# Opening by quarters, filler matmuls in TensorE's waits, and normalized tokens stored in the order in which the gather loads them

## The chip, the cores and the metric

One core of a Trainium2 chip (eight cores, two dies of four) runs the whole kernel. The metric is device time of one execution in microseconds (us), lower is better, as the median of three runs. All inputs lie in HBM and the output goes back there; all arithmetic is fp32, or fp32 split into parts.

## The reference

A decoder trunk of two layers over 256 tokens of width 1024. For each layer:

```python
mod = cond @ w_mod[l] + b_mod[l]                 # cond = silu(c): one row, 6 x 1024 columns
sh1, sc1, g1, sh2, sc2, g2 = split(mod, 6)
h = layer_norm_plain(x) * (1 + sc1) + sh1
q, k, v, p = split(h @ w_in[l], 4)               # 512 columns each
a = moba_attention(rope(q), rope(k), v)          # 256 tokens are one block: causal attention, 8 heads
m = pool_mixer(p, w_pool[l], pool_scale[l])      # trailing means over 2, 4, 8, 16 tokens
x = layer_norm_affine(ALPHA * x + g1 * (concat(a, m) @ w_out[l]), ln1_g[l], ln1_b[l])
h = layer_norm_plain(x) * (1 + sc2) + sh2
y = grouped_moe(h, ...)                          # router, then 2 of 16 SwiGLU experts for each token
x = layer_norm_affine(ALPHA * x + g2 * y, ln2_g[l], ln2_b[l])
```

The weights are some 280 MB in fp32, all read once; the 16 experts of a layer (1024x512 gate and up, 512x1024 down) are the largest part.

## The kernel before

Tokens are held as two halves of 128 partitions (t = 0, 1). All large weights come through one stream (class `Stream`, L35 to L71): a list of pieces in a fixed order, each a DMA of up to 1 MiB issued from the SP queue into a ring of 21 slots of [128, 2048] fp32. A new piece goes out when its slot has been given back; `st.free` in the program says from where on, and on the chip SP waits for the last reader of the slot. Scratch tiles (`slot()`) come from the same ring. The order of every engine's instructions is that of the program (a manual schedule), so an instruction that waits holds up all that stand behind it on its engine. PSUM has eight banks, `ps()`.

A layer runs like this. `mod01` (L301; layer 0) multiplies the conditioning with the columns of shift 1 and scale 1, in two halves h of 512 columns; `mod01_fin` (L314) copies the result, transposes it and adds the biases, which gives columns `col01`. `plain` (L389) normalizes a token half into `xn`; `enter` (L410) transposes xn and applies scale and shift, which gives `hT`. `qk_mm` (L428) multiplies hT with the q and k columns of w_in, for a token half t and a quarter q of the contraction. In layer 0, `ready(h)` does the first three steps for half h and stands before the two quarters that need it (L445). Then `row_parts` (L259) splits rows of constants, and `mod_dve` (L350) forms a modulation row on DVE (VectorE): eight multiply-adds (L356, L358) over [128, 1024]. `rope` (L702) turns parts of q and k on DVE. TensorE (PE) multiplies the pool columns (L478), `pool` (L716) sums windows on POOL (GpSimd), and q and k are transposed (L501) and copied (L502, half of the copies on DVE), scores (L508, L513), softmax, `v` (L552), output projection `out_mm` (L596), `norms_of(t)` (L607) with an affine norm and a plain norm (L391 through `plain`) that writes `xn2[t]`.

The router path follows: `turn(t)` (L620) transposes xn2, logits, `exps`; xn2 is split into `xh` and `xl` (two fp32r parts); `gate()` spreads g2 (L344, L345); `router` picks experts on DVE (L750 to L778), counts places with small matmuls (L784 to L789), and `onehot` (L821) forms the selection matrices. `gather(i)` (L835) then collects the tokens of eight experts: for each k of 8 it multiplies a 128x128 block of xh or xl, taken as the stationary operand with a step of eight columns, with the selection:

```python
T.matmul(b, xs[:, t, k::8], SX[i][t], start=(n == 0), stop=(n == 3))      # L843
```

The experts run as eight pairs (L1035): `gate_up` (L885), `silu`, `act_t` (L905, transposes and an ACT copy), `down` (L922), `combine` (L947). The last pair adds into four banks XB that are kept; statistics of them (L940, L943) stand at the end of `down`, and the closing norm (`norm`, `norm_aside`, L1065 to L1087) is applied in the next layer's `ready` or, at the end, just before the output's DMAs (L1120 to L1123).

## Time and profile before

| | us |
|---|---|
| three runs | 734.01, 729.12, 731.86 (median 731.86) |
| the profiled execution | 732.26 |
| its span on the core | 730.5 |

Over the span PE is busy 675.4 us (92%), DVE 323.9, ACT 127.7, POOL 46.9; the mean DMA rate is 384 GB/s, and HBM reads are 278.59 MB. PE's busy time is no measure of its load: matmuls are pipelined and their ends are modelled. The profile's parts that are used here: the windows view (busy time of each engine, granted TensorE clock, share of the 16 DMA engines and GB/s in a stretch), the timeline (instructions in order of time, with the idle time ahead of each and what ended it), the waits of a queue, and groups by line. PEld is the weight load of a matmul. A granted clock of 1.00 is 2.4 GHz, 0.50 is 1.2 GHz; a value between is a mean over both.

### The profile page before, as it was taken

The page shows a single profiled execution, that of the slowest core. Times are in us where ns is not written, and L with a number is a line of the kernel's source. Part 1 is how long each engine was busy: PE and PEld are TensorE (multiplying, and loading weights), DVE is VectorE, ACT ScalarE, POOL GpSimd, SP SyncE. Part 2 cuts the span into 40 slices and gives each one's busy share as a digit, 9 for nine tenths or more (in the row PEclk, how much of TensorE's full clock was granted, in tenths as well). Part 3 has the DMA queues.
Part 4 walks back from the last instruction along what each step waited for, and adds up shares of the span by engine and source line. Part 5 has one row for each costly group of instructions (what it writes and reads, how often), then busy time and mean ns, then how long its engine had stood idle before and what let it go on. Part 6 is the DMA issues. An engine that isn't in the chain of part 4 may idle for free. (4 is left out here: it accounts for less than half of the span.)

```text
span 730.5 us, 8092 instructions
## 1 busy us (share of the span) xinstructions
PE 675.4 (92%) x3101; PEld 322.0 (44%) x3101; DVE 323.9 (44%) x572; ACT 127.7 (17%) x274; POOL 46.9 (6%) x74
## 2 busy tenths in 40 slices
PE   4899799979899999999979999997999999998994
PEld 1347455544333363333324575555434345332331
DVE  2117898652243343232253876665332342342315
ACT  0111332122001121101102125213210111111100
POOL 4000500100000000000000041010000000000001
PEclk9999899999999999999999999997999999999998
DMA  9999999798999999999999999967599999999992
GB/s 325 395 391 408 410 370 379 282 415 323 423 422 419 421 421 423 421 417 418 398 408 390 409 410 415 372 266 309 216 423 421 422 421 421 421 418 421 418 399 91
DMA packets 57633, 280.36 MB, mean 384 GB/s; under 512 B 5009, under 2 KB 6073, under 8 KB 34537
## 3 DMA queue, kind: packets, MB, share of 16 engines
q1 hardware_dynamic: 56944, 279.20, 94.8%
q8 instruction: 29, 0.48, 0.3%
q10 hardware_dynamic: 312, 0.32, 0.1%
q0 software_dynamic: 320, 0.14, 0.1%
q14 instruction: 28, 0.22, 0.1%
HBM read 278.59 MB, written 1.05 MB: 383 GB/s over the span
## 5 line engine op out<-in xcount | busy, mean ns | idle before, releaser
L885 PE MATMUL ps<-wr 128*64 128x512 f32 x1024 | 224.3, 593 | 0.0
L885 PEld LDWEIGHTS ps<-wr 128*64 128x64 f32 x1024 | 73.1, 137 | 145.6 <-issue 140.7
L922 PE MATMUL ps<-wr,s 128*64 128x512 f32 x512 | 115.3, 602 | 4.0 <-ACT s L910 4.0
L922 PEld LDWEIGHTS ps<-wr,s 128*64 128x64 f32 x512 | 36.1, 138 | 73.3 <-issue 64.0
L932 DVE SCALAR_TENSOR_TENSOR s<-ps,gc,gb 128x512 f32<-128x512 f32 x32 | 23.9, 748 | 89.0 <-PE ps L922 89.0
L434 PE MATMUL ps<-wr,hT 128*128 128x512 f32 x128 | 56.9, 603 | 0.9 <-ACT hT L423 0.6
L596 PE MATMUL ps<-wr,hT 128*128 128x512 f32 (+1 forms) x160 | 55.7, 507 | 0.0
L358 DVE SCALAR_TENSOR_TENSOR wr<-wr,condT 128x1024 f32<-128x1024 f32 x42 | 54.2, 1290 | 2.3 <-DMA wr<-in_w_mod_dram 0.8
L935 ACT CAST wr<-s 128x512 fp32r<-128x512 f32 x30 | 18.5, 618 | 167.1 <-PE ps L885 109.1
L902 DVE TENSOR_TENSOR s<-s,ps 128x512 f32<-128x512 f32 x16 | 11.0, 687 | 79.4 <-PE ps L885 79.4
L936 DVE TENSOR_TENSOR wr<-s,wr 128x512 fp32r<-128x512 f32 x30 | 20.8, 692 | 55.6 <-ACT wr L935 50.8
L596 PEld LDWEIGHTS ps<-wr,hT 128*128 128x128 f32 x160 | 30.2, 190 | 23.8 <-issue 21.3
L434 PEld LDWEIGHTS ps<-wr,hT 128*128 128x128 f32 x128 | 24.4, 194 | 31.0 <-issue 28.5
L947 PE MATMUL ps<-wr,sT 128*128 128x512 f32 x120 | 33.6, 412 | 0.0
L910 ACT COPY s<-ps 128x512 f32<-128x512 f32 x16 | 9.4, 587 | 135.4 <-PE ps L908 135.4
L843 PE MATMUL ps<-s,xn 128*128 128x512 f32 x64 | 28.9, 451 | 2.1 <-DVE s L821 2.1
L1085 POOL TENSOR_TENSOR rs<-rs,mhalf 128x2 f32<-128x2 f32 x2 | 1.4, 702 | 457.1 <-DVE rs L1084 457.1
L552 PE MATMUL ps<-wr,hT 128*128 128x512 f32 x64 | 28.3, 596 | 0.0
L947 PEld LDWEIGHTS ps<-wr,sT 128*128 128x128 f32 x120 | 20.9, 189 | 16.3 <-issue 13.0
L478 PE MATMUL ps<-hT,wr 128*128 128x256 f32 x128 | 28.1, 380 | 0.0
L843 PE MATMUL ps<-s,hT 128*128 128x512 f32 x64 | 27.6, 431 | 0.0
L478 PEld LDWEIGHTS ps<-hT,wr 128*128 128x128 f32 x128 | 24.2, 190 | 4.5 <-issue 1.3
(236 smaller groups left out, 627.2 us busy)
## 6 DMA issues: line engine op xcount, KB each, us to landing
wr<-in_w_gate_dram SPq DMA_DIRECT2D x64, 1024.0 KB, 18.2
wr<-in_w_up_dram SPq DMA_DIRECT2D x60, 1024.0 KB, 18.8
wr<-in_w_down_dram SPq DMA_DIRECT2D x56, 1024.0 KB, 18.7
wr<-in_w_mod_dram SPq DMA_DIRECT2D x48, 1024.0 KB, 14.6
wr<-in_w_in_dram SPq DMA_DIRECT2D x16, 1024.0 KB, 16.7
wr<-in_w_out_dram SPq DMA_DIRECT2D x8, 1024.0 KB, 18.6
wr<-in_w_down_dram SPq DMA_DIRECT2D x12, 512.0 KB, 11.1
wr<-in_w_up_dram SPq DMA_DIRECT2D x8, 512.0 KB, 17.4
```

The lines of the kernel that those rows point to most:

```text
L358: V.scalar_tensor_tensor(acc, w[:, kk], condT[:, k, 0:1], acc, op0=OP.mult, op1=OP.add)
L434: T.matmul(pq[t][n], hT[:, k, t * 128:(t + 1) * 128], w[:, kk, n * 512:(n + 1) * 512], start=(k == 0), stop=(k == 7))
L478: T.matmul(pp[g // 2][:, (g % 2) * 256:(g % 2) * 256 + 256], w[:, kk, g * 128:(g + 1) * 128], hT[:, k, :], start=(k == 0 and g % 2 == 0), ...
L552: T.matmul(pv[t], hT[:, k, t * 128:(t + 1) * 128], w[:, kk, :], start=(k == 0), stop=(k == 7))
L596: T.matmul(py[t][-1][:, 0:c1 - c0], catT[:, k, t * 128:(t + 1) * 128], w[:, kk, n * 512 + c0:n * 512 + c1], start=(q == 2 and kk == 0), st ...
L843: T.matmul(b, xs[:, t, k::8], SX[i][t], start=(n == 0), stop=(n == 3))
L885: T.matmul(bs[nm][64 * j:64 * j + 64, :], XE[i][k // 4][:, k % 4, c0:c0 + 64], st.get((nm, l, 2 * i + j, q))[:, k - k0, :], start=(k == 0) ...
L922: T.matmul(bo[n][64 * j:64 * j + 64, :], AT[i][:, k, 64 * j:64 * j + 64], st.get(("d", l, 2 * i + j, q))[:, k - k0, (n - n0) * 512:(n - n0 ...
L932: V.scalar_tensor_tensor(o, bo[n], GC[i], g2[:, c0], op0=OP.mult, op1=OP.mult)
L935: A.copy(oh[:, c0], o)
L936: V.tensor_sub(ol[:, c0], o, oh[:, c0].bitcast(F))
L947: T.matmul(b, STt[i][:, t * 128:(t + 1) * 128], o[:, n * 512:(n + 1) * 512], start=(start and j == 0), stop=(stop and j == 1), skip_group_ ...
```

## The change

- **Opening by quarters.** The mod01 pieces become four quarters of 256 columns (contiguous runs of 1 KB in HBM where they were 2 KB), each followed by one qk piece; x's second half follows the first quarter. `ready` goes by quarters: mod01 of the next quarter is issued before the second token half of the quarter at hand, and `enter01` transposes both token halves into one bank.
- **Filler matmuls.** `warm(n)` issues n matmuls of constant ones (bf16, 128x512) whose result nobody reads, at eight places, 2 to 10 at a time.
- **Order of xn2.** `norms_of` writes the normalized tokens regrouped (column q*8+k of x goes to place k*128+q), with a strided read on DVE. turn and gather (and `over`) then read runs of 128 columns in place of steps of eight.
- **Smaller moves.** The small loads on POOL's queue come after the constants; mod_dve(2) comes after rope in layer 0; `mod_fin(l+1, 1)` one pair later; act_t of the first and last pair is shared between DVE and ACT; the closing statistics are taken for each token half on its own (`ends(t)`), the second inside the first one's norm.

```diff
     def add_mod01(h):
         w = w_mod[0].rearrange("(p k) n -> p k n", k=8)
-        for q in range(2):
-            for v in range(2):
-                st.add(("m01", h, q, v), w[:, 4 * q:4 * q + 4, v * D + h * 512:v * D + (h + 1) * 512])
+        for v in (1, 0):
+            st.add(("m01", h, v), w[:, :, v * D + h * 256:v * D + (h + 1) * 256])
...
-    for h in range(2):
+    for h in range(4):
         add_mod01(h)
         if not h:
             load_x(1)
-        add_qk(0, 2 * h)
-        add_qk(0, 2 * h + 1)
+        add_qk(0, h)
...
+    def warm(n):
+        b = ps().rearrange("p (a c) -> p a c", a=4)
+        for _ in range(n):
+            T.matmul(b, ones, ones[:, None, :].to_broadcast([128, 4, 128]), start=True, stop=True)
...
     def mod01(h):
         acc = ps()
+        for k in range(8):
             for v in range(2):
+                j = 2 * v + k % 2
+                T.matmul(acc[32 * j:32 * j + 32, 0:256], condT[:, k, :], st.get(("m01", h, v))[:, k, :],
+                         start=(k < 2), stop=(k > 5))
...
+    def enter01(h, hT, xn):
+        b = ps()
+        for k in range(2):
+            for t in range(2):
+                T.transpose(b[:, k * S + t * 128:k * S + (t + 1) * 128],
+                            xn[:, t, (2 * h + k) * 128:(2 * h + k + 1) * 128], ident)
+        return b
+
+    def enter01_fin(h, hT, b):
+        for k in range(2):
+            kk = 2 * h + k
+            o, i = hT[:, kk, :], b[:, k * S:(k + 1) * S]
+            if k:
+                V.tensor_scalar(o, i, colt[0, 1][:, kk:kk + 1], colt[0, 0][:, kk:kk + 1], op0=OP.mult, op1=OP.add)
+            else:
+                A.activation(o, i, AF.Identity, scale=colt[0, 1][:, kk:kk + 1], bias=colt[0, 0][:, kk:kk + 1])
...
-            ready(0)
-            for t in range(2):
-                qk_mm(t, (0, 1))
-            ready(1)
-            qk_mm(0, (2, 3))
+            for q in range(4):
+                if not q:
+                    ready(0)()
+                qk_mm(0, (q,))
+                if q < 3:
+                    fin = ready(q + 1, lambda: qk_mm(1, (q,), (0,)))
+                    qk_mm(1, (q,), (1,))
+                    fin()
...
-        mod_dve(l, 2, acc[2])
         if l:
+            mod_dve(l, 2, acc[2])
             mod_dve(l, 4, acc[4])
         rope(qk)
+        if not l:
+            mod_dve(l, 2, acc[2])
...
-            plain(z, xt[:, t])
+            mv, rs = stats(xt[:, t])
+            V.tensor_scalar(z.rearrange("p (k q) -> p k q", k=8), xt[:, t].rearrange("p (q k) -> p k q", k=8),
+                            mv[:, 0:1], rs, op0=OP.subtract, op1=OP.mult)
...
-                    T.transpose(b[:, k * 128:(k + 1) * 128], xn2[t][:, 4 * h + k::8], ident)
+                    T.transpose(b[:, k * 128:(k + 1) * 128], xn2[t][:, (4 * h + k) * 128:(4 * h + k + 1) * 128], ident)
...
         exps(0)
+        if l + 1 == DEPTH:
+            warm(7)
...
         gate()
+        warm(6)
...
         T.matmul(pc[:, 0:16], ones, M[:, 1], start=False, stop=True)
+        warm(4)
...
-                        T.matmul(b, xs[:, t, k::8], SX[i][t], start=(n == 0), stop=(n == 3))
+                        T.matmul(b, xs[:, t, k * 128:(k + 1) * 128], SX[i][t], start=(n == 0), stop=(n == 3))
...
-            A.copy(a, b.rearrange("p (k s) -> p k s", k=4))
+            bv = b.rearrange("p (k s) -> p k s", k=4)
+            if i in (0, NPAIR - 1):
+                V.tensor_copy(a[:, 0:2], bv[:, 0:2])
+                A.copy(a[:, 2:4], bv[:, 2:4])
+            else:
+                A.copy(a, bv)
...
-        mv2 = tiny.tile([128, 2, 2], F, name="mv2", bufs=1)
-        rs2 = tiny.tile([128, 2], F, name="rs2", bufs=1)
-        for t in range(2):
-            V.bn_aggr(mv2[:, t], bn[t])
-        V.tensor_scalar_add(rs2, mv2[:, :, 1], EPS)
-        P.tensor_tensor(rs2, rs2, mhalf.to_broadcast([128, 2]), op=OP.pow)
-        return [(mv2[:, t], rs2[:, t:t + 1]) for t in range(2)], norm, norm_aside
+        def ends(t):
+            V.bn_stats(bn[t][:, 1, :], XB[t][1])
+            return stats_end(bn[t])
+
+        return ends, norm, norm_aside
...
+            warm(10)
             bias_cols()
-            def ready(h):
-                mod01_fin(h, mod01(h))
-                for t in range(2):
-                    enter(0, t, hT, xn, (h,))
+            def ready(h, between=lambda: None):
+                part = mod01(h)
+                if not h:
+                    warm(2)
+                between()
+                mod01_fin(h, part)
+                b = enter01(h, hT, xn)
+                if not h:
+                    warm(3)
+                return lambda: enter01_fin(h, hT, b)
         else:
             mod_mm(l, 0)
+            warm(3)
+            own = []
             def ready(t):
                 b = tiny.tile([128, 2, 6], F, name="bn")
+                if not t:
+                    own.append(ends(0))
                 for n in range(2):
                     o = xt[:, t, n * 512:(n + 1) * 512]
-                    norm(t, n * 512, (n + 1) * 512, o, *ends[t])
+                    norm(t, n * 512, (n + 1) * 512, o, *own[t])
                     V.bn_stats(b[:, n, :], o)
                 mv, rs = stats_end(b)
-                V.tensor_scalar(xn[:, t], xt[:, t], mv[:, 0:1], rs, op0=OP.subtract, op1=OP.mult)
                 if not t:
                     mod_fin(l, 0)
+                    warm(8)
+                    own.append(ends(1))
+                V.tensor_scalar(xn[:, t], xt[:, t], mv[:, 0:1], rs, op0=OP.subtract, op1=OP.mult)
                 enter(l, t, hT, xn)
...
+    own = [ends(0), None]
+
+    def second():
+        own[1] = ends(1)
+        norm_aside(1, 512, D, rest, *own[1])
+
     for t, a, b in ((0, 0, 512), (0, 512, D), (1, 0, 512)):
-        norm(t, a, b, xt[:, t, a:b], *ends[t], (lambda: norm_aside(1, 512, D, rest, *ends[1])) if t == a == 0 else None)
+        norm(t, a, b, xt[:, t, a:b], *own[t], second if t == a == 0 else None)
         nc.sync.dma_start(out[0, t * 128:(t + 1) * 128, a:b], xt[:, t, a:b])
```

## Rows read from the trace of the kernel before

**Rows 1.** Windows view, us: busy of five engines, granted clock, DMA share, GB/s

```profile
560.00:600.00 40.00, 40.00 (x187) 14.49 (x184) 13.23 (x21) 4.25 (x7) 0.00 (x0) 1.00 1.01 421
90.00:180.00 90.00, 84.80 (x440) 47.76 (x440) 59.43 (x101) 25.16 (x52) 5.15 (x5) 0.98 0.89 353
166.00:176.00 10.00, 10.00 (x47) 4.28 (x48) 3.80 (x12) 3.85 (x5) 0.00 (x0) 1.00 0.66 243
460.00:522.00 62.00, 57.62 (x302) 34.83 (x302) 36.06 (x77) 14.48 (x27) 4.08 (x4) 0.92 0.68 268
```

**Rows 2.** Waits of the DMA queue (SP), 150 to 180: total, times, longest

```profile
SPq L56 <- PE ps L885: 22.4, 3, 18.0
```

**Rows 3.** Timeline, opening, DVE and PE: start, length, instruction, [idle before it, releaser]

```profile
18.16 1.28 DVE L378 BATCH_NORM_STATS2 bn<-xt 128x6 f32<-128x512 f32 x2 [3.31 <-DMA xt<-in_x_dram]
23.14 14.00 PE L434 MATMUL ps<-wr,hT 128*128 128x512 f32 x32 [0.65 <-ACT hT L423]
37.07 3.64 PE L308 MATMUL ps<-wr,condT 128*32 128x512 f32 x32
43.12 14.00 PE L434 MATMUL ps<-wr,hT 128*128 128x512 f32 x32
```

**Rows 4.** Windows view, 8 to 11 us

```profile
8.00:11.00 3.00, 1.02 (x10) 1.02 (x10) 1.26 (x19) 0.00 (x0) 1.98 (x6) 1.00 1.06 370
```

**Rows 5.** Timeline, PE: the transposes of turn(1) in layers 0 and 1

```profile
149.06 1.12 PE L624 MATMUL ps<-ident,wr 128*128 128x128 f32 x8
495.54 1.62 PE L624 MATMUL ps<-ident,wr 128*128 128x128 f32 x8 [1.91 <-DVE wr L391]
```

**Rows 6.** Timeline, 62 to 81 us, DVE, POOL and PE

```profile
62.98 9.21 DVE L358 SCALAR_TENSOR_TENSOR wr<-wr,condT 128x1024 f32<-128x1024 f32 x7
72.10 0.28 DVE L709 TENSOR_TENSOR s<-xn,cs 128x128 f32<-128x128 f32 x1
73.47 2.11 POOL L718 TENSOR_TENSOR wr<-wr 128x1084 f32<-128x1084 f32 x1 [1.03 <-DMA wr<-in_w_mod_dram]
73.64 2.08 DVE L710 TENSOR_TENSOR s<-xn,cs 128x128 f32<-128x128 f32 x1
80.08 0.69 DVE L502 COPY wr<-ps 128x512 f32<-128x512 f32 x1 [0.67 <-PE ps L501]
80.83 2.08 PE L508 MATMUL ps<-wr 64*128 64x128 f32 x16
```

**Rows 7.** Timeline, PE and its weight loads (PEld): gathers and one later group

```profile
156.78 0.18 PE L784 MATMUL ps<-r_M,tri 128*128 128x16 bf16 x1 [2.32 <-DVE r_M L778]
158.11 0.79 PE L843 MATMUL ps<-s,xn 128*128 128x512 f32 x1 [1.05 <-DVE s L821]
162.12 0.33 PEld L843 LDWEIGHTS ps<-s,hT 128*128 128x128 f32 x1
166.77 0.33 PEld L843 LDWEIGHTS ps<-s,xn 128*128 128x128 f32 x1
167.59 4.94 PE L885 MATMUL ps<-wr 128*64 128x512 f32 x22
505.39 0.60 PE L843 MATMUL ps<-s,xn 128*128 128x512 f32 x1 [1.05 <-DVE s L821]
698.70 1.69 PEld L947 LDWEIGHTS ps<-wr,sT 128*128 128x128 f32 x8 [0.81 <-issue]
```

**Rows 8.** Windows view, ahead of and in the gathers

```profile
158.00:162.00 4.00, 3.89 (x10) 3.29 (x11) 0.73 (x2) 0.78 (x1) 0.00 (x0) 0.57 1.01 424
496.00:502.00 6.00, 5.42 (x29) 2.88 (x28) 4.31 (x11) 1.97 (x6) 0.00 (x0) 0.51 1.01 418
```

**Rows 9.** Groups by line, shapes apart: busy, mean ns, idle before, releaser

```profile
L391 DVE TENSOR_SCALAR wr<-xt,mv,rs 128x1024 f32<-128x1024 f32 x4 | 3.3, 813 | 2.8 <-POOL rs L386 2.8
```

**Rows 10.** Timeline, PE, start of layer 1

```profile
384.89 14.90 PE L434 MATMUL ps<-wr,hT 128*128 128x512 f32 x32
```

**Rows 11.** The page's groups: busy, mean ns, idle before

```profile
L1085 POOL TENSOR_TENSOR rs<-rs,mhalf 128x2 f32<-128x2 f32 x2 | 1.4, 702 | 457.1 <-DVE rs L1084 457.1
```

More of the change, by code (lines that the diff above doesn't have):

```diff
@@ L204, in tile_trunk @@
     V.tensor_mul(condT[:, :, 0], th, cc)
-    small_loads()
     wr = const.tile([128, 8, 32], F, name="wr_")
@@ L243, in tile_trunk @@
     V.reciprocal(rcnt, rcnt)
+    small_loads()
     pscol = const.tile([128, 8], F, name="pscol")
@@ L303, in mod01, with mod01_fin @@
         acc = ps()
-        for q in range(2):
-            for kk in range(4):
-                for v in range(2):
-                    j = 2 * v + kk % 2
-                    T.matmul(acc[32 * j:32 * j + 32, :], condT[:, 4 * q + kk, :], st.get(("m01", h, q, v))[:, kk, :],
-                             start=(q == 0 and kk < 2), stop=(q == 1 and kk > 1))
-            for v in range(2):
-                st.free(("m01", h, q, v))
-        return acc
-    def mod01_fin(h, acc):
-        part = s2()
-        A.copy(part, acc)
+        for k in range(8):
+            for v in range(2):
+                j = 2 * v + k % 2
+                T.matmul(acc[32 * j:32 * j + 32, 0:256], condT[:, k, :], st.get(("m01", h, v))[:, k, :],
+                         start=(k < 2), stop=(k > 5))
+        for v in range(2):
+            st.free(("m01", h, v))
+        part = s2(256)
+        A.copy(part, acc[:, 0:256])
+        return part
+    def mod01_fin(h, part):
         b = ps()
-        for k in range(4):
+        for k in range(2):
             T.transpose(b[:, k * 128:(k + 1) * 128], part[:, k * 128:(k + 1) * 128], ident)
-        o = col01[:, :, 4 * h:4 * h + 4]
-        V.reduce_sum(o, b.rearrange("p (k v o r) -> p v k o r", k=4, v=2, o=2)[:, :, :, :, 0], axis=AX.X)
-        V.tensor_add(o, o, bcol[:, 0, 4 * h:4 * h + 4, 0:2].rearrange("p k v -> p v k"))
+        o = col01[:, :, 2 * h:2 * h + 2]
+        V.reduce_sum(o, b[:, 0:256].rearrange("p (k v o r) -> p v k o r", k=2, v=2, o=2)[:, :, :, :, 0], axis=AX.X)
+        V.tensor_add(o, o, bcol[:, 0, 2 * h:2 * h + 2, 0:2].rearrange("p k v -> p v k"))
     def mod_fin(l, v):
@@ L407, in norm_rows, with enter @@
         return ts
-    def enter(l, t, hT, xn, hs=(0, 1)):
-        for h in hs:
+    def enter01(h, hT, xn):
[6 more added lines that the diff above has]
+    def enter01_fin(h, hT, b):
+        for k in range(2):
+            kk = 2 * h + k
[4 more added lines that the diff above has]
+                A.activation(o, i, AF.Identity, scale=colt[0, 1][:, kk:kk + 1], bias=colt[0, 0][:, kk:kk + 1])
+    def enter(l, t, hT, xn):
+        for h in range(2):
             b = ps()
@@ L426, in mixer, with qk_mm @@
         pq = [[ps(), ps()] for _ in range(2)]
-        def qk_mm(t, qs=range(4)):
+        def qk_mm(t, qs=range(4), kks=range(2)):
             for q in qs:
                 w = st.get(("in", l, "qk", q))
-                for kk in range(2):
+                for kk in kks:
                     for n in range(2):
@@ L435, in qk_mm @@
                                  start=(k == 0), stop=(k == 7))
-                if t:
+                if t and 1 in kks:
                     st.free(("in", l, "qk", q))
@@ L453, in mixer @@
             if t:
-                qk_mm(1, range(4) if l else (2, 3))
+                qk_mm(1, range(4) if l else (3,))
             A.activation(qk[:, t, 0:512], pq[t][0], AF.Copy, scale=DH ** -0.5)
@@ L978, in over @@
                         for xs in (xh, xl):
-                            T.matmul(pb[:, k * 128:k * 128 + n], xs[:, t, 4 * h + k::8], Sx[:, t, 0:n],
+                            T.matmul(pb[:, k * 128:k * 128 + n], xs[:, t, (4 * h + k) * 128:(4 * h + k + 1) * 128], Sx[:, t, 0:n],
                                      start=(m == 0), stop=(m == 3))
@@ L1048, in experts @@
                 bs = scatter_t(0)
-                if l + 1 < DEPTH:
-                    mod_fin(l + 1, 1)
             silu(i)
@@ L1058, in experts @@
                 gather(4)
+            if i == 1 and l + 1 < DEPTH:
+                mod_fin(l + 1, 1)
             if more:
```

5 lines of the change are left out of this document (2 added, 3 removed).

## Prediction

> **What bounds the kernel now.** I read the windows view first. From 560 to 600 us the 16 DMA engines are busy all the time (share 1.01) and move 421 GB/s; that is the pace at which the weights come, and in the expert stretches everything else waits for it. So time is lost only where this share falls. From 90 to 180 us it is 0.89: (1.01 - 0.89) x 90 = 10.8 us of DMA time are lost there, 3.5 of them in the last hole (166 to 176 at 0.66). In layer 1 it is 0.68 from 460 to 522, a loss of 20.5 us [rows 1]. The waits of the DMA queue say why: SP waits 18.0 us in one piece for L885, the first expert matmul, to give back a ring slot [rows 2]. The ring is full, the next transfer needs a slot, and the slot comes when TensorE gets to the experts. So whatever makes L885 start earlier in a layer moves all later transfers earlier by as much, until that layer's holes are used up. Work that ends sooner inside a saturated stretch brings nothing.
>
> The sum is therefore the shift of L885 in layer 0, plus that in layer 1, plus what happens after the last weight. It is made on the profiled execution, 732.26 us (span 730.5 and 1.8 around it); the median of the three runs is 731.86, 0.4 below.
>
> **Opening.** Before, DVE gets the second token half's x at 18.16, behind 5.24 MB (two halves of x, four pieces of 1.05 MB); the first qk matmul (L434) starts at 23.14, 4.98 later, that time being statistics, xn, biases and hT. Then TensorE runs through: 32 matmul passes in 14.0 us, the second mod01 3.64, 32 more from 43.12, so qk ends at 57.12 [rows 3]. After, x1 stands behind one quarter, 2.10 MB less. In the stretch where only mod01's pieces (2 KB runs) come the DMA moves 370 GB/s [rows 4], against 421 with the experts' 8 KB runs [rows 1]. Per engine that is 88 and 311 ns a run, so 37 ns a KB and 14 a run, which puts the 1 KB runs of the quarters, shown by no row, at 51 ns or 320 GB/s. At best they keep 370, at worst the fixed part is larger than the line says (rival 3); I take the line through the two rows. The 2.10 MB less save 5.7 us and the 2.10 MB that stay cost 0.9 more: x1 lands at 13.4, qk starts at 18.4. TensorE still has 28.0 of qk, three later quarters of mod01 at 1.82 (half of 3.64) and per quarter six transposes, about 0.9 (eight take 1.12 [rows 5]): 36.2. ACT's copy and DVE's columns lie under the 1.75 us halves of qk_mm(1, q). One wait is left: the second quarter's weights land at 13.4 + 2.6 (a qk piece) + 6.6 = 22.6 and TensorE asks for them at 21.9. qk ends at 55.3, 1.8 earlier. All 8.39 MB of mod01 cost the DMA 26.2 instead of 22.7 us: 3.5, paid out of the 10.8.
>
> One rule speaks on this. The Trainium skill's page "DMA: Bandwidth & Descriptors", Specifications, gives 512 B as the size from which a transfer has line rate. The trace disagrees: 2 KB runs are 12% below 8 KB runs [rows 4, 1]. By the rule the 1 KB runs would cost nothing more (rival 4 has that case).
>
> **Order on DVE in layer 0.** Before, mod_dve(2) goes first, rope behind it and into POOL's pooling: a rope step of 0.28 takes 2.08 behind POOL's add of 2.11; then the q copies, and the scores (L508) start at 80.83, 23.7 after qk [rows 6]. After: mod_dve's second product, before 5.9 after qk's end, comes 3.4 later, behind twelve rope steps of 0.28, and seven products take 9.21: 55.3 + 5.9 + 3.4 + 9.2 = 73.8. POOL's add, 16.35 after qk, is due at 71.65 and gets in ahead of the last product: 2.1 more, 75.9. Two copies of 0.69 and the scores start at 77.3: 3.5 earlier. Bounds: 5.6 if POOL does not get in, 1.7 if qk does not end earlier. From the scores on TensorE and DVE hand work back and forth up to out_mm, so the 3.5 holds.
>
> **Gather.** Before, from 158.11 to 167.59, 9.48 us for 32 matmuls [rows 7]. TensorE had waited 2.3 us ahead of L784 and 1.05 ahead of L843 [rows 7], and the granted clock is 0.57 over 158 to 162 [rows 8]: mostly the 1.2 GHz level, then 2.4. At the full level weight loads follow at (166.77 - 162.12) / 19 = 0.245. Unstrided loads of the same 128x128 size (L947) take 0.19, and eight come in 1.69, so (1.69 - 0.19) / 7 = 0.214 [rows 7]. 32 x (0.245 - 0.214) = 1.0. If the clock stays up, another 9.48 - 32 x 0.245 = 1.6. warm(6) and warm(4), at some 0.24 each, lie in those two waits; at the low level (twice that) the second would stick out by 0.9. So 2.6 together; bounds 0 and 2.6, and I take 2.6, because the fillers leave at most 0.9 us of each wait idle.
>
> So layer 0 gives 3.5 + 2.6 = 6.1; the 10.8 - 3.5 = 7.3 of DMA slack cover it, and the last hole's 3.5 covers the gather's part.
>
> **Layer 1.** Gather again 2.6 (same instructions). From turn to gather TensorE runs at granted 0.51 (496 to 502), the 1.2 GHz level, having waited 1.9 us on DVE: from 495.54 to the gather at 505.39 it takes 9.85, where layer 0 takes 9.05 (149.06 to 158.11) [rows 5, 7, 8]. warm(7) lies in that wait: 0.8 gained. Against it stands the write of xn2 in the new order, on this path in layer 1 (in layer 0 TensorE's turn does not wait for it [rows 5]). It takes 0.81 with unit steps [rows 9]. No DVE read in steps of 32 bytes stands in the trace. Nearest is TensorE's load: 0.33 strided, 0.19 not, a factor of 1.75 [rows 7]. Bounds are 0 and, at twice that factor, 2.0; I take 0.81 x 0.75 = 0.6, less 0.1 for transposes that now read unit steps: 0.5.
>
> The Trainium skill's page "SBUF — State Buffer", Door 1, says that accesses that each go to a new 16-byte line pay a penalty, and that free steps end at four fp32. TensorE's 0.33 against 0.19 agrees. It speaks against this part: the stride is moved from TensorE to DVE, not removed.
>
> At the seam between the layers L434's first 32 passes take 14.90 [rows 10] against 14.00: 0.9 to get from warm(3) and warm(8). But ends(1) now lies on DVE ahead of xn: a statistic of 0.64 [rows 3] and two small operations, an estimated 0.5 together, less the wait on POOL's power of 0.70 [rows 11] that they fill. I take 0.5 lost. Net 0.4, bounds -0.5 and 0.9. Layer 1: 2.6 + 0.8 - 0.5 + 0.4 = 3.3, of 20.5 lost.
>
> **End.** The two halves' powers were one POOL instruction of 0.70 [rows 11], covered by the first subtraction. Now the second half's comes after it, in front of DVE's nb, with nothing to cover it and the first output write queued behind: 0.8 lost with its aggregate. Splitting the last act_t copy can give a part of one ACT copy; taken at nothing, as w_down still streams in then.
>
> Sum: 6.1 + 3.3 - 0.8 = 8.6. 732.26 - 8.6 = 723.7, by the median 723.3: **723 us**. The other edits (constants ahead of small_loads, mod_fin(1, 1) one pair later, act_t of pair 0) lie where x1's landing or the DMA ends the wait; uncovered, each would be under 1 us.
>
> **Rivals.**
> 1. The clock is not held: fillers too short or too early. The 1.6 twice, 0.8 and 0.9 go, 4.9: 728.6. For it: up to 0.9 us idle beside the fillers. Against: most of each wait is filled. 0.20.
> 2. The opening ends no sooner, because TensorE waits in every quarter: scores 1.7 earlier only, 725.5. 0.13.
> 3. The other side, slower: 1 KB runs at 200 GB/s. Then mod01 takes 42.0 us, 19.3 more; 10.8 is slack, 8.5 is not: 732.3 + 8.5 - 2.5 = 738.3. It decides from 233 GB/s down, where 13.3 more eat the slack and the 2.5 of layer 1 and the end. Against: the line from two run lengths would have to miss by a third. 0.07.
> 4. 1 KB runs are as fast as 2 KB runs (370 GB/s): x1 at 12.5, no wait at the second quarter, qk ends at 53.7, scores 5.1 earlier: 722.1. The DMA page's rule is this case. Or POOL does not get in: scores 5.6 earlier, layer 0 capped by its slack of 7.3: 722.5. Together 0.10.
>
> **How the numbers follow.** Forecast 0.50, within 720 to 726. Range: 718, below rivals 4, to 730, above rival 1; rival 3 and the edges are left out. A measurement of this kernel tells about 1% from no change, so faster means below 724.5: 0.43 of the forecast, 0.10 of rivals 4, 0.05 of rival 2 and 0.03 of rival 1: 0.61. Slower is rival 3: 0.07. The rest is 0.32.
>
> **What would show it.** L434's first start near 18, its last end near 55; L508 near 77; the gather in 6.9 us with no stretch near 0.5, loads 0.19 long; L885 6 earlier in layer 0; that layer's last DMA hole nearly gone; L391's strided form near 1.4; some 320 GB/s while mod01's pieces come. The prediction is wrong if L885 moves and the span does not (the DMA not the bound), or if TensorE waits for mod01's pieces in every quarter.

## The result, and the profile after

Four runs of the changed kernel took 723.43 to 724.93 us, median **724.12**; the kernel before, run beside it, has a median of 732.93 (four runs). The ratio is 0.9895, 95% interval 0.9863 to 0.9926: some 1% faster. The forecast was 723 (718 to 730), so the time and the direction came as predicted. The profiled execution took 724.93 (span 723.1), 7.3 less than that of before (732.26), where the sum had 8.6. The terms of that sum are another matter: the opening and the order on DVE were too small, the gather was too large, and the seam between the layers had the wrong sign.

The stretches and the DMA queue first: windows view of the changed kernel (us, busy of PE, PEld, DVE, ACT, POOL, granted clock, DMA share, GB/s), then SP's waits from 150 to 180.

```profile
8.00:11.00 3.00, 3.00 (x15) 1.35 (x13) 1.80 (x5) 0.00 (x0) 1.72 (x3) 1.00 1.12 345
90.00:180.00 90.00, 86.28 (x463) 45.39 (x465) 57.24 (x99) 21.87 (x42) 5.21 (x5) 1.00 1.00 403
151.00:155.00 4.00, 3.83 (x17) 2.62 (x16) 2.07 (x3) 0.86 (x2) 0.00 (x0) 1.00 1.00 424
370.00:380.00 10.00, 7.51 (x34) 3.24 (x31) 4.06 (x12) 0.67 (x2) 1.53 (x2) 0.66 1.02 403
460.00:522.00 62.00, 58.56 (x341) 32.18 (x341) 34.92 (x75) 14.98 (x28) 4.14 (x4) 1.00 0.68 269
```

```profile
SPq L56 <- PE ps L918: 22.8, 4, 15.0
```

The DMA share of 90 to 180 has gone from 0.89 to 1.00 [rows 1]: the holes of layer 0 are nearly used up. In layer 1 it is 0.68 as before. The granted clock, 0.57 and 0.51 in the stretches of [rows 8], is 1.00 in the gather (151 to 155) and over 460 to 522; it has a new dip at the start of layer 1, 0.66 from 370 to 380 (0.50 from 372 to 378), where the kernel before has 1.00 over 370 to 380. SP still waits for the first expert matmul, now L918, 15.0 us where it was 18.0 [rows 2].

The timeline of the opening and of DVE up to the scores (start, length, engine, line):

```profile
13.03 1.29 DVE L381 BATCH_NORM_STATS2 bn<-xt 128x6 f32<-128x512 f32 x2 [1.61 <-DMA xt<-in_x_dram]
18.09 3.70 PE L455 MATMUL ps<-wr,hT 128*128 128x512 f32 x8 [0.20 <-ACT hT L429]
22.02 1.93 PE L311 MATMUL ps<-wr,condT 128*32 128x256 f32 x32 [0.24 <-DMA wr<-in_w_mod_dram]
45.54 8.75 PE L455 MATMUL ps<-wr,hT 128*128 128x512 f32 x20
...
62.07 0.28 DVE L745 TENSOR_TENSOR xn<-s 128x128 f32<-128x128 f32 x1
63.05 10.82 DVE L361 SCALAR_TENSOR_TENSOR wr<-wr,condT 128x1024 f32<-128x1024 f32 x7
70.63 2.16 POOL L749 TENSOR_TENSOR wr<-wr 128x1084 f32<-128x1084 f32 x1 [1.03 <-ACT wr L513]
73.79 1.27 DVE L528 COPY wr<-ps 128x512 f32<-128x512 f32 x2
74.62 2.08 PE L534 MATMUL ps<-wr 64*128 64x128 f32 x16 [3.48 <-DVE wr L528]
```

x's second half is there at 13.03 (18.16 before), qk starts at 18.09 and ends at 54.29; the scores start at 74.62, 6.2 earlier than in [rows 6].

The router's end and the gather in layer 0, and the same part of layer 1:

```profile
150.48 0.18 PE L816 MATMUL ps<-r_M,tri 128*128 128x16 bf16 x1 [1.07 <-DVE r_M L810]
150.62 1.02 PE L283 MATMUL ps<-ones 128*128 128x512 bf16 x4
151.81 0.47 PE L876 MATMUL ps<-s,xn 128*128 128x512 f32 x1 [0.17 <-DVE s L854]
155.40 0.19 PEld L876 LDWEIGHTS ps<-s,xn 128*128 128x128 f32 x1
159.34 13.95 PE L918 MATMUL ps<-wr 128*64 128x512 f32 x64
...
488.04 1.67 PE L283 MATMUL ps<-ones 128*128 128x512 bf16 x7
489.29 1.20 DVE L646 TENSOR_SCALAR wr<-xt,mv,rs 128x1024 f32<-128x1024 f32 x1 [0.73 <-POOL rs L389]
490.63 1.06 PE L653 MATMUL ps<-ident,wr 128*128 128x128 f32 x8 [0.92 <-DVE r_mx L713]
499.55 0.47 PE L876 MATMUL ps<-s,xn 128*128 128x512 f32 x1 [0.17 <-DVE s L854]
507.08 13.10 PE L918 MATMUL ps<-wr 128*64 128x512 f32 x60
```

The gather takes 159.34 - 151.81 = 7.53 us (9.48 before) and the same 7.53 in layer 1; its loads last 0.19 in place of 0.33 [rows 7]. L918 of layer 0 starts 8.25 earlier than L885 did. L646, the strided write, takes 1.20 where L391 took 0.81 [rows 9].

Then the seam between the layers, where part of this is given back. Two lines of the kernel before, then the changed kernel:

```profile
379.42 1.07 PE L293 MATMUL ps<-wr,condT 128*32 128x512 f32 x8 [1.18 <-DMA wr<-in_w_mod_dram]
382.33 0.81 DVE L1112 TENSOR_SCALAR xn<-xt,mv,rs 128x1024 f32<-128x1024 f32 x1 [0.73 <-POOL rs L386]
...
369.19 1.07 PE L297 MATMUL ps<-wr,condT 128*32 128x512 f32 x8 [1.15 <-DMA wr<-in_w_mod_dram]
372.74 1.93 PE L297 MATMUL ps<-wr,condT 128*32 128x512 f32 x8 [2.49 <-DMA wr<-in_w_mod_dram]
374.61 1.46 PE L283 MATMUL ps<-ones 128*128 128x512 bf16 x3
375.86 1.06 PE L335 MATMUL ps<-ident,s 128*128 128x128 f32 x4
376.96 0.17 DVE L337 TENSOR_REDUCE col<-ps 128x8 f32<-128x16 f32 x1 [5.62 <-PE ps L335]
377.26 0.69 DVE L1118 BATCH_NORM_STATS2 bnx<-ps 128x6 f32<-128x512 f32 x1
378.30 0.80 DVE L1162 TENSOR_SCALAR xn<-xt,mv,rs 128x1024 f32<-128x1024 f32 x1
380.43 14.00 PE L455 MATMUL ps<-wr,hT 128*128 128x512 f32 x32
```

The last piece of m(1,0), shift 1 of layer 1, is multiplied at 372.74; in the kernel before that was at 379.42, so 6.7 of the 8.25 us arrive here. From there to the first qk matmul it takes 7.69 us, before 384.89 - 379.42 = 5.47 ([rows 10] has the 384.89): 2.2 lost. Two things are in these 7.69. DVE sits idle for 5.62 us because L1162 (xn), which once stood ahead of mod_fin, now stands behind mod_fin's reduction L337 and ends(1); what xn itself reads was there some 5 us before (xn_first, below, starts it at 371.28). And TensorE has waited 2.49 and the clock is at its 1.2 GHz level: the matmuls of that last piece take 1.93 in place of 1.07, and warm(3), issued behind them, takes 1.46 and holds up the transposes L335. mod_first, below, has the same order here and needs 5.87; the mean granted clock over the way is 1.00 there and 0.63 here. So 1.8 of the 7.69 are the clock's fall. What is left is 0.4 above the kernel before, whose 5.47 hold some 0.4 of a lower clock of their own (0.87; from its transposes to qk it takes 1.60, in mod_first 1.21): at the full clock the new order costs 0.4 to 0.8. It shows as so little because in the kernel before xn was late as well, 2.9 us behind the start of that last piece (382.33).

The end of the program, two lines of the kernel before and then the changed kernel:

```profile
719.55 0.70 DVE L943 BATCH_NORM_STATS2 bnx<-ps 128x6 f32<-128x512 f32 x1
725.93 0.97 DVE L1070 SCALAR_TENSOR_TENSOR xt<-xt,rs,wr 128x512 f32<-128x512 f32 x1
...
711.50 0.70 DVE L1118 BATCH_NORM_STATS2 bnx<-ps 128x6 f32<-128x512 f32 x1
714.47 0.55 POOL L389 TENSOR_TENSOR rs<-rs,mhalf 128x1 f32<-128x1 f32 x1 [1.15 <-DVE rs L388]
715.05 0.16 DVE L1112 SCALAR_TENSOR_TENSOR nb<-mv,rs 128x1 f32<-128x1 f32 x1 [0.72 <-POOL rs L389]
718.61 0.97 DVE L1107 SCALAR_TENSOR_TENSOR xt<-xt,rs,wr 128x512 f32<-128x512 f32 x1
```

DVE waits 0.72 us for POOL's second power, as the prediction had it; from the statistic L1118 (L943 before) to the last norm it is 7.11 us, before 6.38.

### The profile page after: what moved, and what is told of

Same layout as the page of the kernel before. It is cut to its first block, busy times and chain, and to the rows that moved or that the text cites. A ratio compares the mean times of both kernels' runs of the same rounds, so it can differ in the third digit from the quotient of the medians.

```text
span 723.1 us, 8334 instructions
## 1 busy us (share of the span) xinstructions
PE 678.9 (94%) x3213; PEld 316.8 (44%) x3218; DVE 326.8 (45%) x582; ACT 124.8 (17%) x268; POOL 49.7 (7%) x76
## 5 line engine op out<-in xcount | busy, mean ns | idle before, releaser
L918 PE MATMUL ps<-wr 128*64 128x512 f32 x1024 | 226.1, 596 | 0.0
L918 PEld LDWEIGHTS ps<-wr 128*64 128x64 f32 x1024 | 73.5, 138 | 147.2 <-issue 142.3
L960 PE MATMUL ps<-wr,s 128*64 128x512 f32 x512 | 113.8, 595 | 3.7 <-DVE s L945 2.9
L361 DVE SCALAR_TENSOR_TENSOR wr<-wr,condT 128x1024 f32<-128x1024 f32 x42 | 55.8, 1329 | 2.3 <-DMA wr<-in_w_mod_dram 0.9
L389 POOL TENSOR_TENSOR rs<-rs,mhalf 128x1 f32<-128x1 f32 x16 | 13.2, 823 | 554.1 <-DVE rs L388 554.1
L933 DVE SCALAR_TENSOR_TENSOR s<-s,ps 128x512 f32<-128x512 f32 x16 | 11.0, 685 | 36.7 <-ACT s L932 36.7
L876 PE MATMUL ps<-s,xn 128*128 128x512 f32 x64 | 25.4, 398 | 0.3 <-DVE s L854 0.3
L996 DVE TENSOR_TENSOR xt<-xt,ps 128x512 f32<-128x512 f32 x40 | 25.2, 683 | 0.5
```

The lines of the kernel that those rows point to most:

```text
L361: V.scalar_tensor_tensor(acc, w[:, kk], condT[:, k, 0:1], acc, op0=OP.mult, op1=OP.add)
L876: T.matmul(b, xs[:, t, k * 128:(k + 1) * 128], SX[i][t], start=(n == 0), stop=(n == 3))
L918: T.matmul(bs[nm][64 * j:64 * j + 64, :], XE[i][k // 4][:, k % 4, c0:c0 + 64], st.get((nm, l, 2 * i + j, q))[:, k - k0, :], start=(k == 0) ...
L960: T.matmul(bo[n][64 * j:64 * j + 64, :], AT[i][:, k, 64 * j:64 * j + 64], st.get(("d", l, 2 * i + j, q))[:, k - k0, (n - n0) * 512:(n - n0 ...
L996: V.tensor_add(b if i == NPAIR - 3 else xt[:, t, c0], xt[:, t, c0], b)
```

## The experiments

Each kernel was timed beside the kernel before; medians are over 4 to 12 runs. In us, from one profiled execution of each: start of the first expert matmul of layer 0, of the last quarter of m(1,0), of layer 1's qk, of its experts; then the span, the median of the runs, and the ratio to the kernel before with its 95% interval.

| kernel | experts 0 | m(1,0) | qk 1 | experts 1 | span | median | ratio |
|---|---|---|---|---|---|---|---|
| before | 167.59 | 379.42 | 384.89 | 514.98 | 730.5 | 732.93 | 1 |
| changed | 159.34 | 372.74 | 380.43 | 507.08 | 723.1 | 724.12 | 0.9895 (0.9863 to 0.9926) |
| changed_again | 159.46 | 371.80 | 379.43 | 506.10 | 721.9 | 723.67 | 0.9887 (0.9849 to 0.9924) |
| opening_alone | 165.75 | 378.81 | 382.93 | 514.27 | 729.6 | 729.73 | 0.9960 (0.9940 to 0.9981) |
| mod_first | 162.79 | 374.06 | 379.93 | 506.60 | 723.1 | 725.07 | 0.9906 (0.9875 to 0.9937) |
| runs_2k | 158.37 | 370.57 | 377.56 | 504.23 | 720.1 | 722.52 | 0.9865 (0.9831 to 0.9898) |
| no_fillers | 160.98 | 373.32 | 380.67 | 508.77 | 725.1 | 727.06 | 0.9927 (0.9903 to 0.9952) |
| stride_8 | 160.06 | 371.45 | 378.79 | 505.75 | 722.9 | 724.13 | 0.9873 (0.9846 to 0.9900) |
| xn_first | 160.16 | 372.57 | 377.83 | 505.88 | 722.3 | 723.81 | 0.9875 (0.9844 to 0.9905) |
| joined | 158.59 | (373.24) | 376.63 | 503.29 | 718.7 | 720.94 | 0.9843 (0.9817 to 0.9869) |
| joined_again | 159.58 | (372.83) | 376.22 | 504.55 | 720.3 | 722.26 | 0.9881 (0.9842 to 0.9921) |
| joined_filled | 160.79 | (375.73) | 379.12 | 505.79 | 721.2 | 720.83 | 0.9850 (0.9828 to 0.9873) |

changed_again is the changed kernel once more. In brackets: there the quarter waits for transposes issued ahead of it. Two profiled executions of the same changed kernel differ by about 1 us from m(1,0) on, so the columns tell differences of 1.5 or more, not less. The kernel before, timed beside each, had medians of 730.71 to 733.44, so medians of different rows are compared only roughly; the ratios leave this out.

**opening_alone.** The opening put into the kernel before, with its own fillers and the later small loads, nothing else (the shortened diff shows the stream; `ready` and its helpers are as in the change).

```diff
-    for h in range(2):
+    for h in range(4):
         add_mod01(h)
...
-        add_qk(0, 2 * h)
-        add_qk(0, 2 * h + 1)
+        add_qk(0, h)
```

> The kernel before, with the opening by quarters alone (pieces of 256 columns in 1 KB runs, the new ready, the fillers inside the opening, small loads after the constants); order on DVE, order of xn2, router, seam and end as before the change. Theory A (a lead ahead of the experts of layer 0 counts as far as that layer's DMA has holes): qk ends about 2.8 earlier as in the changed kernel, scores and the first expert matmul as much; the runs of 1 KB cost the DMA some 2.1 us, the holes held 10.8, so all 2.8 are passed on: about 2.8 below the kernel before (733.4), 730.6. Theory B (the DMA is full from the first weight on, and what the short runs cost is paid at the end): 2.8 - 2.1 = 0.7 below. Theory C (mod_dve or POOL sets the scores, not qk): scores where they were, no gain, or 2.1 lost.

Measured 729.73, 0.4% below the kernel before: Theory A's 730.6 lies within the interval, Theory B's 0.7 below (a ratio of 0.9990) and Theory C's outside. Its profiled execution ends only 0.9 earlier (it is one of the kernel's longer ones, 731.42), with qk from 18.62 to 55.23 and the scores at 78.94, 1.9 earlier, where Theory A had 2.8. At the start of layer 1, where this kernel has no fillers, qk's first passes (a pass is one 128x512 matmul) run at the full clock all the same:

```profile
382.93 14.00 PE L455 MATMUL ps<-wr,hT 128*128 128x512 f32 x32
```

**mod_first.** The order on DVE in layer 0 undone.

```diff
+        mod_dve(l, 2, acc[2])
         if l:
-            mod_dve(l, 2, acc[2])
             mod_dve(l, 4, acc[4])
         rope(qk)
-        if not l:
-            mod_dve(l, 2, acc[2])
```

> The changed kernel with one part undone: in layer 0 the eight products of mod_dve(2) stand ahead of rope again, as before the change. In the changed kernel the first expert matmul of layer 0 (L918) starts 8.25 us earlier than before the change, but the last piece of m(1,0), the weights at the end of that layer's stream, lands only 6.7 earlier. Theory A: layer 0 passes on a lead only as far as its DMA had holes, 6.7 us; what L918 gains beyond that is worth nothing. Here the scores should start 23.7 after qk's end as before the change, at 54.3 + 23.7 = 78.0 in place of 74.6; L918 then starts 3.4 later, 4.9 earlier than before the change, and the time rises only by 6.7 - 4.9 = 1.8, to about 726. Theory B: every us of L918's lead counts and the rest was lost in other places: 3.4 longer, 727.5. Theory C: the order on DVE does not matter, because POOL's adds hold DVE up either way: within 0.5 of 724.1.

The scores start at 78.04, as worked out, and the first expert matmul 3.45 later. The median is 725.07, 1 to 1.4 above the changed kernel's two: nearer to Theory A's 726 than to Theory B's 727.5, though the interval of the ratio reaches up to 728. But the reason in Theory A is not what the table shows. m(1,0) comes 1.3 to 2.3 later, and the seam then takes back 1.8:

```profile
374.06 1.07 PE L297 MATMUL ps<-wr,condT 128*32 128x512 f32 x8 [1.48 <-DMA wr<-in_w_mod_dram]
379.93 14.00 PE L455 MATMUL ps<-wr,hT 128*128 128x512 f32 x32
```

TensorE waits 1.48 for this quarter in place of 2.49, its matmuls take 1.07 at the full clock, and qk follows after 5.87 in place of 7.69. The order of the seam's instructions is the same in both, so this 1.8 is what the clock's fall costs there. Over all kernels of the table up to xn_first the way from the first expert matmul to m(1,0) is 211.3 to 213.4 us and does not grow with the lead; a limit of 6.7 us on the lead is not shown. Of the 3.45 the seam takes back 1.8; the rest goes on the way to m(1,0), and why is open.

**runs_2k.** The quarters of mod01 in 2 KB runs (the columns of the modulation then belong to other weights, as its expectation says).

```diff
-            st.add(("m01", h, v), w[:, :, v * D + h * 256:v * D + (h + 1) * 256])
+            st.add(("m01", h, v), w[:, 4 * (h % 2):4 * (h % 2) + 4, v * D + (h // 2) * 512:v * D + (h // 2 + 1) * 512])
...
-                T.matmul(acc[32 * j:32 * j + 32, 0:256], condT[:, k, :], st.get(("m01", h, v))[:, k, :],
+                T.matmul(acc[32 * j:32 * j + 32, 0:256], condT[:, k, :], st.get(("m01", h, v)).rearrange("p a (b c) -> p (a b) c", b=2)[:, k, :],
```

> The changed kernel, with mod01's quarters read as 2 KB runs (four rows of 512 columns in place of eight of 256): the same bytes in pieces of the same size and order. The columns then stand in the wrong quarters, so shift 1 and scale 1 of layer 0 come from other weights; all else is computed as in the changed kernel. While mod01's pieces come the changed kernel moves 365 to 387 GB/s where the kernel before moved 391 to 398: about 0.9 MB less from 10 to 50 us, 2.1 us at 421 GB/s. Theory A (layer 0's lead is limited by its DMA time): L918 starts about 0.8 earlier, m(1,0) lands 2 us earlier and the time falls by 2 to about 722. Theory B (what TensorE gains ahead of L918 is all that counts): x1 lands some 0.7 earlier, the time falls by about 0.8, to 723.3. Theory C: runs of 1 KB cost nothing against 2 KB: no difference, and the same GB/s in the opening.

```profile
10.00:50.00 40.00, 37.75 (x230) 18.68 (x229) 7.66 (x21) 3.75 (x8) 1.83 (x4) 1.00 1.07 373
10.00:50.00 40.00, 38.18 (x232) 18.71 (x231) 7.66 (x21) 4.34 (x9) 1.46 (x4) 1.00 1.04 387
```

Windows view of the changed kernel and of runs_2k: 373 and 387 GB/s over 10 to 50 us. The median of 722.52 is 1.2 to 1.6 below the changed kernel: between Theories A and B, their intervals overlap, and which of the two it is stays open. Theory C falls: 1 KB runs do cost, 14 GB/s here, or 40 us x 14 / 421 = 1.3 us of DMA time.

**no_fillers.**

```diff
-        if l + 1 == DEPTH:
-            warm(7)
...
-        warm(6)
...
-        warm(4)
```

> The changed kernel without the filler matmuls at L723, L781 and L822 (ahead of turn(1) in layer 1, and in the router's two waits of both layers); those of the opening and of the seam stay. If the fillers hold the clock, the gather's first part runs at the 1.2 GHz level again and takes about 9.1 in place of 7.5 us in each layer, and turn to gather in layer 1 takes 0.9 longer. Theory A (layer 0's lead beyond 6.7 us is worth nothing): layer 0's 1.6 only uses up L918's 8.25, so the loss is layer 1's 0.9 + 1.6 = 2.5: about 726.6. Theory B (every us counts): 0.9 + 1.6 + 1.6 = 4.1: about 728.2. Theory C: the clock stays up without them, since TensorE now waits less: gather 7.5, no difference.

The median rises by 2.9 to 3.4 us (2.3 to 2.9 by the ratios): the fillers work, and Theory C falls. Between A's 726.6 and B's 728.2 the 727.06 does not decide, and the 0.9 that both put in for turn to gather did not come. Windows and timeline of no_fillers in layer 1:

```profile
500.00:502.00 2.00, 2.00 (x6) 1.54 (x6) 0.18 (x1) 0.23 (x1) 0.00 (x0) 0.50 0.72 303
```

```profile
490.78 1.09 PE L653 MATMUL ps<-ident,wr 128*128 128x128 f32 x8 [2.35 <-DVE wr L646]
499.72 0.72 PE L872 MATMUL ps<-s,xn 128*128 128x512 f32 x1 [1.05 <-DVE s L850]
```

Without them the gather begins at the 1.2 GHz level and takes 508.77 - 499.72 = 9.05 in place of 7.53 (8.77 in layer 0). But turn(1) runs at the full clock after a wait of 2.35, and from there to the gather it is 8.94 us, with warm(7) 8.92. So the 0.9 that was won there against the kernel before is not shown to come from warm(7). What the fillers are shown to give is the gathers' 1.2 and 1.5 us.

**stride_8.** The order of xn2 undone.

```diff
-            mv, rs = stats(xt[:, t])
-            V.tensor_scalar(z.rearrange("p (k q) -> p k q", k=8), xt[:, t].rearrange("p (q k) -> p k q", k=8),
-                            mv[:, 0:1], rs, op0=OP.subtract, op1=OP.mult)
+            plain(z, xt[:, t])
...
-                        T.matmul(b, xs[:, t, k * 128:(k + 1) * 128], SX[i][t], start=(n == 0), stop=(n == 3))
+                        T.matmul(b, xs[:, t, k::8], SX[i][t], start=(n == 0), stop=(n == 3))
...
```

> The changed kernel with the order of xn2 undone: the second normalization writes 1024 columns in a row, turn and gather read with a step of eight columns; fillers and all else as changed. Theory A: at the full clock the gather's loads come every 0.245 us in place of 0.227, so the gather takes 8.1 in place of 7.5 in each layer; layer 0's 0.6 is within the lead that is worth nothing, layer 1 loses 0.6 and wins back 0.4 because the write takes 0.81 in place of 1.22: about 0.2 longer, 724.3. Theory B (the strided read slows more than the loads): gather above 8.5 us in each layer, time up by 1 or more. Theory C: the stride costs TensorE nothing at the full clock and the write on DVE is pure loss: gather 7.5 and the time 0.4 shorter.

```profile
155.10 0.33 PEld L874 LDWEIGHTS ps<-s,hT 128*128 128x128 f32 x1
...
159.25 0.33 PEld L874 LDWEIGHTS ps<-s,xn 128*128 128x128 f32 x1
```

The gather takes 8.15 in both layers (160.06 - 151.91 in layer 0) and the median is 724.13: Theory A, and the rewritten order is worth nothing that can be measured. With the clock up, the strided loads last 0.33 but still follow each other every (159.25 - 155.10) / 17 = 0.244; without the stride 0.227. The 0.6 us that this gives a gather goes against 0.4 more in the write.

**xn_first.**

```diff
             mod_mm(l, 0)
-            warm(3)
...
+                V.tensor_scalar(xn[:, t], xt[:, t], mv[:, 0:1], rs, op0=OP.subtract, op1=OP.mult)
                 if not t:
-                    mod_fin(l, 0)
-                    warm(8)
                     own.append(ends(1))
-                V.tensor_scalar(xn[:, t], xt[:, t], mv[:, 0:1], rs, op0=OP.subtract, op1=OP.mult)
+                    mod_fin(l, 0)
```

> The changed kernel with another order at the start of layer 1: xn of the first token half and ends(1) stand ahead of mod_fin(1,0), and warm(3) and warm(8) are left out. In the changed kernel xn waits on DVE behind mod_fin's reduction, and so for the last piece of m(1,0): that lands at 372.7, its matmuls take 1.93 at the 1.2 GHz level, the column reduction comes at 376.96, ends(1) 377.26, xn 378.30, transposes 379.28, first qk matmul 380.43. Theory S: the order costs; xn is done by 373, only the transposes, ACT's scale and the reduction stand between the landing and qk, which starts near 377.6, 2.9 earlier; qk's first part then runs at the 1.2 GHz level for 0.9: the time falls by about 2, to 722.1. Theory D: qk waits for the weights of m(1,0) whichever order there is, and losing the fillers costs as much as the order gives: 724 to 725.

```profile
371.28 0.81 DVE L1157 TENSOR_SCALAR xn<-xt,mv,rs 128x1024 f32<-128x1024 f32 x1 [0.73 <-POOL rs L389]
372.57 1.93 PE L297 MATMUL ps<-wr,condT 128*32 128x512 f32 x8 [2.46 <-DMA wr<-in_w_mod_dram]
377.83 15.38 PE L455 MATMUL ps<-wr,hT 128*128 128x512 f32 x32
```

xn is done at 372.1, qk starts 5.26 after the last quarter in place of 7.69, as Theory S has it; but the clock stays low, its first 32 passes take 15.38 in place of 14.00, and of 2.4 us 1.0 is left. The median, 723.81, is just under Theory D's 724 to 725 and 1.7 above Theory S's 722.1. So the order alone is worth little while the clock is low; the next kernels change both.

**joined**, and **joined_again** beside **changed_again** on one chip. The seam with both, the new order and fillers in the wait, and the closing statistics ahead of the first norm (shortened; `enter` is divided into its transposes, `enter_t`, and the rest, `enter_e`).

```diff
-            mod_mm(l, 0)
-            warm(3)
+            mod_mm(l, 0, (0, 1, 2))
+            warm(8)
...
-                if not t:
-                    mod_fin(l, 0)
-                    warm(8)
-                    own.append(ends(1))
                 V.tensor_scalar(xn[:, t], xt[:, t], mv[:, 0:1], rs, op0=OP.subtract, op1=OP.mult)
-                enter(l, t, hT, xn)
+                if t:
+                    enter(l, t, hT, xn)
+                    return
+                own.append(ends(1))
+                bs = [enter_t(t, h, xn) for h in range(2)]
+                mod_mm(l, 0, (3,))
+                mod_fin(l, 0)
+                for h in range(2):
+                    enter_e(l, t, h, hT, bs[h])
...
-    own = [ends(0), None]
+    own = [ends(0), ends(1)]
```

> The changed kernel with two places written anew. Start of layer 1: xn of the first token half and ends(1) come ahead of mod_fin, the transposes of xn are issued ahead of the last quarter of m(1,0), and warm(8) stands in TensorE's wait for that quarter (warm(3) left out). End: the statistics of both token halves are taken before the first norm, so that POOL's two powers lie beside DVE's work. Theory A: the seam's order cost; from the landing at 372.7 only the last quarter (1.07 at the full clock), ACT's copy, four transposes, two small DVE operations and the first scale are left, so qk starts near 376.5 in place of 380.4 and runs 14.0; with 0.6 at the end the time falls by about 4.5, to 719.6. Theory L: layer 1's weights hold the work up (mod_dve(1,2) starts with its weights 24.6 after m(1,0)'s landing in every run so far, whatever qk does), so the seam gives at most the 1 us that it gave when only the order of xn was changed, and the time is 722.5. Theory E: the end's 0.6 does not show, because the output's DMAs wait for each other: the last norm ends 0.6 earlier but the span does not.

> The changed kernel itself, on one chip beside the kernel with the new seam and end. Theory A: the layer 0 lead ends at the landing of m(1,0) and the seam's order lost 3 to 4 us of it; median near 724, and the new seam and end are worth 3 to 4 us beside it. Theory N: the 3.2 us between the two medians so far are a difference of chips; the two come out within 1 us of each other.

> The kernel with xn, ends(1) and the transposes ahead of the last quarter of m(1,0), warm(8) in the wait for it, and both statistics ahead of the first closing norm, once more, beside the changed kernel on one chip. Theory A: near 721, 3 to 4 us below the changed kernel, with qk of layer 1 starting about 3.4 us after that quarter's first matmul in place of 7.7. Theory N: within 1 us of the changed kernel.

```profile
372.25 1.06 PE L442 MATMUL ps<-ident,xn 128*128 128x128 f32 x8 [1.71 <-DVE xn L1166]
373.24 1.07 PE L299 MATMUL ps<-wr,condT 128*32 128x512 f32 x8
375.01 0.66 PE L337 MATMUL ps<-ident,s 128*128 128x128 f32 x4 [0.71 <-ACT s L332]
...
376.22 15.70 PE L463 MATMUL ps<-wr,hT 128*128 128x512 f32 x32 [0.96 <-ACT hT L452]
```

(Three lines of joined, the last of joined_again.) In joined's trace qk starts at 376.63 as worked out and its first 32 passes take 14.00; the experts of layer 1 start 3.8 earlier than in the changed kernel, the span is 4.4 shorter, and from the same closing statistic to the last norm it is 6.45 again. From the start of that norm to the end of the span it is 4.6, in the changed kernel 4.5, so the span does follow the norm and Theory E falls. Theory L's limit falls too: the weights of mod_dve(1,2) are there at 398.91 in joined_again and at 398.95 in changed_again, yet the experts of layer 1 start 1.55 earlier. The medians are less clear: 720.94 for joined, but 722.26 for joined_again beside changed_again's 723.67, with runs from 720.98 to 725.74 and 721.29 to 725.22. In joined_again's trace qk's first passes took 15.70: the granted clock had fallen to 0.72 over 376 to 382. Whether the two kernels are 1 us apart or 3 is settled by neither set.

**joined_filled.** The change is shown against joined.

```diff
-            warm(8)
+            warm(14)
...
                 mod_mm(l, 0, (3,))
+                warm(2)
                 mod_fin(l, 0)
+                warm(3)
```

> The kernel with the new seam and end, with more fillers in the seam's waits: warm(14) for warm(8) ahead of the transposes of xn, warm(2) after the last quarter of m(1,0), warm(3) after mod_fin's transposes. Theory K: what spreads the runs of one kernel is where the granted clock falls to the 1.2 GHz level; without these fillers the first 32 passes of layer 1's qk took 14.0 in one profiled execution (span 718.7, mean clock 0.992) and 15.7 in another (720.3, 0.989). With the waits filled the clock does not fall there: qk's first 32 passes take 14.0, the mean clock is at least 0.990 in all runs and they lie within 2 us of each other around 720.5. Theory N: the spread has other causes (the DMA, the chip); the runs spread over 3 us or more as those of the changed kernel do, around 721.7.

The six runs are 719.92 to 722.98, median 720.83, ratio 0.9850 (0.9828 to 0.9873); five of them lie at 721.66 or below, where one of ten runs of the changed kernel does. qk's first passes take 14.00. The seam is as Theory K has it; the mean clock is 0.990 to 0.992 in five runs, and 0.988 in the sixth, the profiled one, which lost its time in the opening (the first eight qk matmuls took 4.67 in place of 3.70). Over all six the spread is 3.1 us, which is Theory N's; without the profiled one it is 1.7. So that the fillers narrow the spread is not shown. By the medians it is 2.8 to 3.3 us below the changed kernel, and not to be told from joined (720.94).

## Why the prediction came out, step by step

**What bounds the kernel: right.** An earlier first expert matmul moved the transfers that follow, 6.7 of 8.25 us as far as m(1,0), and the holes of 90 to 180 shrank with it: by (1.01 - share) x 90 from 10.8 us to 0.9 in the changed kernel; 8.1 in opening_alone (share 0.92), 4.5 in mod_first (0.96), 2.7 in no_fillers (0.98).

**Opening: right in kind, too cautious in size.** x1 at 13.03 (13.4 predicted), qk from 18.09 (18.4), one wait for a quarter of 0.24 (0.7). The line through two run lengths gave 320 GB/s for 1 KB runs; it is 345 in the stretch of [rows 4], and the loss against runs_2k is 1.3 us of DMA time over 10 to 50 us (1.9 over 4 to 50, 367 against 384 GB/s), not 3.5. qk ends 2.8 earlier in place of 1.8. Rival 3 needed 233; rival 4's first half, no cost at all, falls with runs_2k, its second with POOL's 1.6 us below. The rule of the Trainium skill, "DMA: Bandwidth & Descriptors", Specifications, that 512 B suffice for line rate, does not hold here: at the same place in the same kernel 1 KB runs move 373 and 2 KB runs 387 GB/s.

**Order on DVE: right, 2.7 us too small.** Forecast for the scores was 77.3, measured 74.62: 1.0 from qk's end; 0.5 because mod_dve's second product starts 8.8 after that, not 9.3; 0.5 because POOL's add inside the seven products costs 10.82 - 9.21 = 1.6 and not its whole 2.1; and some 0.6 because the scores start behind the first of DVE's two copies (74.62, the two end at 75.06).

**Gather: right in cause, 0.6 too large.** 1.95 and 2.06 measured, 2.6 predicted. The clock part is there (no_fillers). The pitch of the loads is 0.227, not 0.214. Eight loads of L947 at 0.214 were the wrong row for it; they too alternate with 512-column matmuls, and why they follow closer is open.

**Layer 0 together** was to give 6.1; the first expert matmul came 8.25 earlier.

**Seam: the step that failed.** The prediction put +0.4: 0.9 from qk's clock, -0.5 for ends(1) ahead of xn. The 0.9 came (14.00 for 14.90), but opening_alone, with no filler at the seam, has 14.00 as well, so it is not shown to be the fillers' work. The way to qk became 2.2 longer, not 0.5. What the step left out is TensorE's wait for the last weights: 1.18 us in the kernel before, 2.49 here. The clock was low behind it, and warm(3) and warm(8) came too late: 1.8 us, by mod_first. The 0.5 for the order is near the 0.4 to 0.8 that are left at the full clock, but by luck: it priced the operations that were put ahead of xn (a statistic and two small ones), and not the wait that came with them. mod_fin's reduction, now ahead too, waits for the weights that land last, and this shows as so little only because xn was late before as well. Against a seam with xn ahead the same order costs 2.4 (7.69, and 5.26 in xn_first, which also leaves the fillers out).

**Layer 1 else: right in sum.** Turn to gather 0.93 gained (0.8 predicted), but not shown to be warm(7)'s work. The strided write took 1.21 (1.3 to 1.4 predicted), 0.4 of loss in place of 0.5. The Trainium skill's "SBUF — State Buffer", Door 1, by which an access that goes to a new 16-byte line each time pays, agrees twice: the write has 1.21 against 0.81, the load 0.33 against 0.19. stride_8 shows no difference in the time from the two together.

**End: right.** 0.73 lost, 0.8 predicted; joined gets 0.66 back. What the other edits are worth (act_t divided, mod_fin(1, 1) one pair later) no run shows.

In numbers of the profiled executions: 6.7 at m(1,0), -2.2 and +0.9 at the seam, -0.5 up to turn(1), +0.9 and +2.1 to the experts, about +0.1 on the way, -0.7 at the end: 7.3. The forecast's 723 stood on errors that cancel: layer 0 underrated by 2.2, of which 1.6 were gone again at m(1,0) (0.5 in the other execution; why they differ is open), the seam overrated by 1.7, layer 1's gather by 0.5.

**The rivals.** Rival 1 priced the clock at 4.9, 4.0 of it for the places that no_fillers empties; that run gives 2.9 to 3.4, because turn to gather did not fall back and the gathers lost 1.2 and 1.5, not 1.6 each. The clock did fall in one place, the seam, because the fillers came too late, which the rival did not have. Rival 2 fell with the 0.24. Rival 3, the one that ended slower, fell with the 345 GB/s.

## What to carry to other kernels

An operation that is moved takes on the waits of everything it now stands behind: price the latest landing among them, not the lengths of the operations. A lead won early in a kernel is worth what arrives at the next place that waits for the last weights, so read the wait there, and the clock behind it, before adding up terms. Put fillers into the wait itself, ahead of the instruction that waits: behind it, as at this seam, they came too late. In the wait they were no guarantee either: joined_again had them there and lost the clock one step later.
